# RWKV-7 chunk products on whole 128x128 tiles of TensorE, and a shorter top-k bit step

## The chip, the cores and the metric

The kernel runs on one core of one Trainium2 chip. The metric is the device time of one execution in microseconds (us); the figure given is a median over runs of the same program.

## What is computed

One layer of a hybrid encoder, for a prompt of 1024 frames and a sample of 64 frames with history. One projection of the normed input (1024 columns to 5836) feeds three branches: A, RWKV-7 time mixing with 8 heads of 64; B, forgetting attention with 8 heads; C, sparse attention whose top-k keys are picked by an indexer. The gated branches are projected back and added. The change touches branch A and the top-k of branch C. Branch A is, per head and frame:

```python
def step(S, inp):
    r_t, w_t, k_t, v_t, kk_t, a_t = inp
    sa = jnp.einsum('bhij,bhj->bhi', S, -kk_t)
    S = (S * w_t[:, :, None, :] + sa[..., None] * (kk_t * a_t)[:, :, None, :]
         + v_t[..., None] * k_t[:, :, None, :])
    return S, jnp.einsum('bhij,bhj->bhi', S, r_t)
```

followed by a group norm per head. Top-k keeps, per query row, the 256 best scores (144 for the sample).

## The kernel before

The kernel is one program in the Tile framework, which orders the instructions of each engine; the source gives the order by generators that are woven together.

The early stage normalises the input, loads constants (`setup`, L270) and runs the indexer, which produces the scores. The projection of every 128 columns (a piece) is `proj` (L148): 8 steps of three matmuls for each of three spans of frames. Weights come by `load_w` (L122): a transfer on SyncE's queue into one of two raw buffers (`NW=2`), a cast by ScalarE, then six GpSimd operations. Pieces are filler: `pump` (L190) advances them by credits after every step of other work. `park_mixed` (L759) is the filler that blends each column with the frame before it, through a row `zs`.

The long stage is branch A. Frames are cut in chunks of 64; a unit is four chunks of one pair of heads. There are 17 units, 16 of the prompt and one of the sample. `braid` (L236) interleaves, for unit u, by the declared step counts: the tail of u-2 (group norm and gate), the chain of u-1, the inverse and the value rows of u, and the preparation of u+1. After every step it pumps 0.7 of a filler step. Beside it top-k advances 17 steps a unit.

In `prepare` the elementwise part (L1268) loads the unit's rows by four transfers, then forms decayed queries and keys (QR, BK). `chunk_rows` (L1359) turns BK, forms the products of keys and queries for each head with a contraction of 64 (L1384) and masks them into BN (the strictly lower part) and BA. `chunk_invert` (L1464) inverts a unit triangular matrix of 64x64 per head and chunk. It doubles the block size five times; a level has one group of whole products (`whole`, L1450) and one or two groups of eight 64x64 products (`each`, L1443), and both the inverse U and its transpose T are updated by VectorE. A last correction step gives UD. `chain` (L1507) walks the four chunks: old state times queries (L1531), UD times that (L1536), both heads' rows copied to UV, the new state (L1544, L1549), and the output rows (L1553, L1555). Each of these is issued once per head, on 64 rows or 64 columns of the array.

`topk` (L546) finds a threshold per row bit by bit, 32 times: four small VectorE operations make the candidate (L581, L570, L571, L583), ScalarE and VectorE count the scores above it, and three more (L591 to L593) settle the bit.

After the stage come the attention branches with the rest of the projections and the output projection as filler. An fp32 matmul appears as two rows in the trace, one for each pass.

## Time and profile before

| What | Value |
| --- | --- |
| Runs | 1340.92 us median of 3 (1340.4 to 1344.45) |
| Profiled execution | 1340.06 us; its span, first to last instruction, 1338.3 us |
| TensorE matmul busy | 1268.5 us, 95% |
| TensorE weight load busy | 966.5 us, 72% |
| VectorE busy | 863.3 us, 65% |
| ScalarE busy | 776.4 us, 58% |
| GpSimd busy | 671.9 us, 50% |
| Mean granted TensorE clock | 0.978 |

Busy time is the union of an engine's rows. A matmul row runs until its modelled end, and rows overlap, so what a matmul costs in the queue is read from the start of one to the start of the next. PEld rows are weight loads and overlap matmuls. A line number is that of the kernel before; a helper's line covers all its callers.

### The profile page before, as it was taken

How to read it: one execution, taken by the hardware profiler on the slowest of the kernel's cores; microseconds unless marked ns; L12 is line 12 of the kernel's file. 1: busy time of each engine (PE TensorE's matmuls, PEld its weight loads, DVE VectorE, ACT ScalarE, POOL GpSimd, SP SyncE). 2: the span in 40 equal slices, each digit the busy share in tenths (PEclk: the TensorE clock that was granted, in tenths of full speed). 3: DMA queues.
4: the chain of work that ended last, by engine and by line, in shares of the span. 5: the costliest groups of instructions: out<-in, count | busy, mean ns of one | idle time of the engine just before them, and what ended most of it. 6: DMA issues, size and time to landing. Idle time of an engine off the chain costs nothing.

```text
span 1338.3 us, 29487 instructions
## 1 busy us (share of the span) xinstructions
PE 1268.5 (95%) x10563; PEld 966.5 (72%) x10563; DVE 863.3 (65%) x2603; ACT 776.4 (58%) x1758; POOL 671.9 (50%) x975
## 2 busy tenths in 40 slices
PE   7799999999999999999899998999999989999997
PEld 5567677777777676677666776888888766777764
DVE  7338437878777777767995316556666489666642
ACT  6234437676777677676353346667665477555532
POOL 6224355454454455555454465656666566444411
PEclk9999999999999899989999999999999989999999
DMA  7351523223223223424232469777664576543323
GB/s 222 68 106 46 152 86 94 66 61 94 62 70 113 91 79 111 144 92 120 69 104 67 155 172 261 223 210 214 181 202 131 169 215 180 138 131 99 99 76 95
DMA packets 172622, 169.61 MB, mean 127 GB/s; under 512 B 38546, under 2 KB 147130, under 8 KB 172475
## 3 DMA queue, kind: packets, MB, share of 16 engines
q1 hardware_dynamic: 172314, 166.89, 43.1%
q8 instruction: 84, 1.38, 0.4%
q0 software_dynamic: 160, 0.82, 0.3%
q14 instruction: 64, 0.52, 0.1%
HBM read 104.61 MB, written 62.24 MB: 125 GB/s over the span
## 4 chain that ended last, share of the span: by engine, by line
PE 72%; DVE 12%; DMA 7%; ACT 3%; issue 3%; POOL 2%; SPq 1%; DVEq 0%; POOLq 0%; ACTq 0%
PE pproj L154 32%; PE pproj L1669 6%; PE ps_pv L966 4%; PE ps_atp L107 4%; PE ps_tp L1669 4%; DMA wraw<-in_w_in_dram 3%; PE ps_ga L1384 3%; PE ps_sc L935 2%; PE ps_sc L936 2%; PE ps_gb L1443 2%; PE ps_gc L1553 1%; PE ps_tp L107 1%; PE ps_gb L1450 1%; PE ps_gc L1555 1%; ACT junka L587 1%
## 5 line engine op out<-in xcount | busy, mean ns | idle before, releaser
L154 PE MATMUL pproj<-uH,wh 128*128 128x384 f32 (+4 forms) x1088 | 496.5, 456 | 0.0
L154 PE MATMUL pproj<-uH,wl 128*128 128x384 f32 (+4 forms) x1088 | 364.7, 335 | 0.0
L154 PE MATMUL pproj<-uL,wb 128*128 128x384 bf16 (+4 forms) x1088 | 360.8, 332 | 0.0
L154 PEld LDWEIGHTS pproj<-uH,wh 128*128 128x128 f32 (+1 forms) x1088 | 218.4, 201 | 4.1
L154 PEld LDWEIGHTS pproj<-uH,wl 128*128 128x128 f32 (+1 forms) x1088 | 209.2, 192 | 2.1
L154 PEld LDWEIGHTS <-wb 128*128 128x128 bf16 (+1 forms) x1088 | 106.8, 98 | 116.9 <-issue 80.2
L587 ACT ACTIVATE junka<-score,tk_ntau 128x1024 f16<-128x1024 f32 (+4 forms) x160 | 149.3, 933 | 42.3 <-DVE tk_ntau L583 21.6
L887 POOL TENSOR_SCALAR S<-S,mx 128x128 f32<-128x128 f32 (+8 forms) x136 | 102.7, 759 | 83.3 <-DVE mx L886 63.2
L140 POOL TENSOR_TENSOR wl<-wraw,wh 128x256 fp32r<-128x256 f32 (+1 forms) x184 | 138.0, 780 | 10.5 <-ACT wh L137 9.9
L905 DVE TENSOR_TENSOR hl<-ps_atp,hl 128x512 fp32r<-128x512 f32 (+3 forms) x184 | 109.4, 600 | 51.0 <-ACT hl L904 49.4
L904 ACT CAST hl<-ps_atp 128x512 fp32r<-128x512 f32 (+3 forms) x184 | 93.1, 514 | 68.9 <-PE ps_atp L107 61.8
L882 ACT ACTIVATE S<-S,mx 128x128 f32<-128x128 f32 (+8 forms) x136 | 105.7, 778 | 44.9 <-DVE mx L878 40.4
L142 POOL TENSOR_SCALAR wb<-wraw 128x512 bf16<-128x512 f32 (+1 forms) x92 | 61.4, 683 | 126.9 <-issue 57.2
L966 PE MATMUL ps_pv<-hl,VS 128*128 128x256 f32 (+3 forms) x640 | 113.9, 291 | 5.8 <-ACT hl L904 2.5
L966 PEld LDWEIGHTS ps_pv<-hl,VS 128*128 128x128 f32 (+1 forms) x640 | 89.6, 175 | 18.9 <-ACT hl L904 3.6
L107 PE MATMUL ps_atp<-ident,S 128*128 128x128 f32 x616 | 102.7, 277 | 0.4 <-POOL S L887 0.2
L1132 POOL TENSOR_TENSOR cb<-nm,T 128x256 f32<-128x256 bf16 (+2 forms) x80 | 51.5, 649 | 62.7 <-DVE mx L878 52.7
L107 PEld LDWEIGHTS ps_atp<-ident,S 128*128 128x128 f32 x616 | 75.4, 142 | 5.7 <-POOL S L887 0.6
L1669 PE MATMUL pproj<-oh,gh 128*128 128x512 f32 x144 | 69.3, 500 | 0.4 <-ACT pproj L1717 0.3
L137 ACT CAST wh<-wraw 128x1024 fp32r<-128x1024 f32 (+1 forms) x46 | 47.7, 1037 | 34.8 <-PE pproj L154 28.0
L776 DVE SCALAR_TENSOR_TENSOR zm<-pproj,omm,zs 128x384 f32<-128x384 f32 (+2 forms) x52 | 25.8, 495 | 45.5 <-ACT zs L775 42.3
L1669 PE MATMUL pproj<-ol,gb 128*128 128x512 bf16 (+1 forms) x144 | 52.8, 387 | 1.7 <-DVE ol L1649 1.7
(377 smaller groups left out, 2889.5 us busy)
## 6 DMA issues: line engine op xcount, KB each, us to landing
wraw<-in_w_in_dram SPq DMA_DIRECT2D x45, 512.0 KB
oraw<-in_w_out_dram SPq DMA_DIRECT2D x12, 512.0 KB
out_dram<-rows SPq DMA_DIRECT2D x10, 512.0 KB
x<-in_x_prompt_dram SPq DMA_DIRECT2D x8, 512.0 KB
wt<-a_wa SPq DMA_DIRECT2D x16, 256.0 KB
b_v<-vs SPq DMA_DIRECT2D x8, 512.0 KB
VS<-b_v SPq DMA_DIRECT2D x8, 512.0 KB
d_y<-y SPq DMA_DIRECT2D x64, 64.0 KB
```

The source lines that it names most:

```text
L107: self.nc.tensor.transpose(out, x, self.ident[:n, :n])
L140: nc.gpsimd.tensor_tensor(l[:, k:k + 2, :n], raw[:, k:k + 2, :n], h[:, k:k + 2, :n], op=OP.subtract)
L142: nc.gpsimd.tensor_scalar(b[:, k:k + 4, :n], raw[:, k:k + 4, :n], 1.0, 0.0, op0=OP.mult, op1=OP.add)
L154: self.nc.tensor.matmul(ps[:n, :nt], a[:, k, :n], b[:, k, t0:t0 + nt], start=(k == 0 and i == 0), stop=(k == KD - 1 and i == 2))
L587: nc.scalar.activation(junk[:, :sc.shape[1]], sc, AF.Sign, bias=ntf[:, j:j + 1], accum_out=cnt[:, j:j + 1])
L882: nc.scalar.activation(S[:, :kn], S[:, :kn], AF.Exp, bias=mx[:, nm - 1:nm], scale=-1.0, accum_out=mx[:, 6:7])
L887: nc.gpsimd.tensor_scalar(S[:, :kn], S[:, :kn], mx[:, 7:8], 0.5, op0=OP.mult, op1=OP.mult)
L904: nc.scalar.copy(ph[:kr, a:b], ps[:kr, a:b])
L905: nc.vector.tensor_tensor(pl[:kr, a:b], ps[:kr, a:b], ph[:kr, a:b], op=OP.subtract)
L966: nc.tensor.matmul(pv[0:m, q0:256], VS[:, kb, 0:m], hl[:, x, o:o + w], start=kb == 0 and x == 0, stop=at[-1][0] == last and n == 3)
L1132: nc.gpsimd.tensor_tensor(o, x, y, op=OP.add)
L1669: nc.tensor.matmul(ps[hf][:n, :], parts[m // 4][q][:, m % 4, :n], self.wo[m][q // 2][:, hf * 512:hf * 512 + 512], start=m == 0 and q == 0, ...
```

## The change

Both heads of a pair are placed on the diagonal of one 128x128 stationary tile (zeros elsewhere), so that one whole product replaces two on halves. For that there are three QB buffers and U0, zeroed once, and masks of 128 columns. The inverse keeps only U and turns it after each level by a product with an identity (`transposed`), so it yields 18 times instead of 14. The chain issues one product for the old state, one for the inverse, two for new state and output rows together, one for the output part of the old state; the state is then updated per half, and the output rows are added per half at the end. Value rows and the tail turn two chunks at once. A unit's four loads can be issued while the unit before is prepared (`elem_loads`, `ahead`), with one buffer for `wt` and `zt`. There is one raw weight buffer (`NW=1`), with a separate one for the first piece. `park_mixed` works in rows of one span and fetches the last column of the span before from its projection bank. Top-k keeps the threshold in sign-corrected form and settles a bit in three operations. The value-row product (L1429) stays on 64x64 tiles.

```diff
@@ load_w
-        raw = self.wraw.tile([P, KD, P], F32, tag="raw", name="wraw")
+        pool, wide, x = (self.wsp, P, "") if self.loaded else (self.ip, n, "0")
+        raw = (self.wraw if self.loaded else pool).tile([P, KD, wide], F32, tag="raw" + x, name="wraw")
...
-NW=2
+NW=1
@@ setup
+            for con, a, b in ((xa, 0, D), (xc, D, C_M)):
+                nc.sync.dma_start(out=con[:, :b - a], in_=I["consts"][:, a:b])
+                nc.vector.tensor_copy(self.con[:, a:b], con[:, :b - a])
...
+            for c in (slice(0, 64), slice(64, P)):
+                nc.sync.dma_start(out=lrows[0:8, c], in_=I["a_lnx_w"].rearrange("x (a p) -> (x a) p", p=64))
+                nc.sync.dma_start(out=lrows[8:16, c], in_=I["a_lnx_b"].rearrange("x (a p) -> (x a) p", p=64))
@@ topk
         for b in range(31, -1, -1):
-            bit = 1 << b
-            v.tensor_scalar(cand, cur, bit if b < 31 else -2147483648, None, op0=OP.bitwise_xor)
-            to_float(cand)
-            v.tensor_scalar(ntau, tau, -2147483648, None, op0=OP.bitwise_xor)
             for j in range(na):
...
-            v.tensor_tensor(ge, cnt, k1, op=OP.is_ge)
-            v.tensor_scalar(t1, ge, float(bit) if b < 31 else -2147483648.0, None, op0=OP.mult)
-            v.tensor_tensor(cur, cur, t1, op=OP.bitwise_xor)
+            v.tensor_tensor(ge, cnt, k1, op=OP.is_lt)
...
+                v.tensor_scalar(t1, ge, float(1 << b), float(1 << b - 1 if b else 0), op0=OP.mult, op1=OP.add)
+                v.tensor_tensor(tau, tau, t1, op=OP.bitwise_xor)
@@ park_mixed
+        last = None
         for t0, n in CHUNKS:
             ps = yield from self.proj(w, t0, n)
+            zs = self.zs.tile([P, 388], F32, tag="zs", name="zs")
+            if last is None:
+                v.memset(zs[:, 0:1], 0.0)
+            else:
+                nc.scalar.activation(zs[:, 0:1], last, AF.Copy, scale=mu)
+            last = ps[:, n - 1:n]
@@ prepare, elem
         yield from self.elem(self.one, slots, x)
+        if after and all(f"a{hp}" in self.filled for hp, _ in after):
+            self.ahead = self.elem_loads(after)
         yield from self.chunk_rows(self.one, x)
...
+        rb = tile("e1", "rb")
+        sc.copy(rb.rearrange("p (x o) -> p x o", x=4), rn.rearrange("p (x o) -> p x o", o=1).broadcast_to([P, 4, 64]))
         for b in range(2):
-            for h in range(2):
-                rb = rn[:, 2 * b + h:2 * b + h + 1].broadcast_to([P, 64])
-                nc.tensor.matmul(ps[halves[h], b * P:b * P + P], rb, self.ident, start=True, stop=True)
+            nc.tensor.matmul(ps[:, b * P:b * P + P], rb[:, b * P:b * P + P], self.ident, start=True, stop=True)
...
+        for h in range(2):
+            v.tensor_tensor(BK[hv[h], :, h], r3(tha)[hv[h]], Pi[hv[h]], op=OP.mult)
+            g.tensor_tensor(BK[hv[h], :, 1 - h], r3(kp)[hv[h]], Pi[hv[h]], op=OP.mult)
+            v.tensor_tensor(QB[hv[h], :, 1, h], kk[hv[h]], Pt[hv[h], :, 0:64], op=OP.mult)
+            g.tensor_tensor(QB[hv[h], :, 0, 1 - h], r3(r)[hv[h]], Pt[hv[h], :, 1:65], op=OP.mult)
@@ chunk_rows
+        for c0 in (0, 2):
             ps = G()
+            for c in (0, 1):
+                nc.tensor.matmul(ps[:, 256 * c:256 * c + 256], BK[:, c0 + c].rearrange("p a t -> p (a t)"),
+                                 QB[:, c0 + c].rearrange("p x h t -> p (x h t)"), start=True, stop=True)
+            q = ps.rearrange("p (c x h t) -> p x h c t", c=2, x=2, h=2)
+            for i, dst in ((1, BN[:, :, c0:c0 + 2]), (0, A[:, :, 2 * c0:2 * c0 + 3:2])):
+                for h in range(2):
+                    v.tensor_tensor(dst[:, h], q[:, i, h], am[:, i].broadcast_to([P, 2, 64]), op=OP.mult)
@@ chunk_invert
+        def thin(*pairs):
+            ps = G()
             for c in range(4):
                 for i, (l, r) in enumerate(pairs):
+                    nc.tensor.matmul(ps[:, c * 64:c * 64 + 64], l(c), r(c), start=i == 0, stop=i == len(pairs) - 1)
...
+        def wide(l, r):
+            ps = G()
+            for c in range(4):
+                nc.tensor.matmul(ps[:, c * P:c * P + P], flat(l[:, c]), flat(r[:, c]), start=True, stop=True)
...
         for lv in range(5):
+            Y = on_diagonal(thin((nd[0], lambda c: T[:, c])), C_LV + 128 * lv)
             yield
-            if lv < 4:
-                pt = each(at(U), at(Y))
-                T2 = t16("T16", 2)
-                v.tensor_tensor(T2, T, pt, op=OP.subtract)
-                T = T2
-            pu = each(at(Y), at(U))
-            U2 = t16("U16", 2)
+            pu = wide(Y, U)
+            U2 = diag("U16", bufs=2)
             v.tensor_tensor(U2, U, pu, op=OP.subtract)
             U = U2
             yield
+            T = transposed(U)
+            yield
@@ chain
-            for h in range(2):
-                nc.tensor.matmul(pa[hv[h]], QR[hv[h], c, 1], S[hv[h]], start=True, stop=True)
+            nc.tensor.matmul(pa, flat(QB[:, c, 1]), S, start=True, stop=True)
...
+            nc.tensor.matmul(pb, flat(UD[:, c]), za, start=True, stop=True)
...
             for h in range(2):
+                nc.tensor.matmul(ch[:, h, c], BA[:, h, c], UV[:, h, c], start=True, stop=True)
...
             for h in range(2):
+                v.scalar_tensor_tensor(self.state[hv[h]], ch[hv[h], h, c], Pt[hv[h], c, 64:65], sp[hv[h]], op0=OP.mult, op1=OP.add)
+            nc.tensor.matmul(ab[:, 256 + c * 64:320 + c * 64], flat(QB[:, c, 0]), S, start=True, stop=True)
...
+        sc.copy(Yt, ab[:, 256:512].rearrange("p (c t) -> p c t", t=64))
+        for h in range(2):
+            o = hv[1 - h]
+            v.tensor_tensor(Yt[o], ch[o, h], Yt[o], op=OP.add)
@@ program
-                work.append(("invert", s.chunk_invert(s.one, x[u]), 14, ()))
+                work.append(("invert", s.chunk_invert(s.one, x[u]), 18, ()))
```

## Rows read from the trace of the kernel before

**Rows 1.** Stages: us, then busy us (count) of each engine, clock, DMA.

```profile
166.00:433.00 267.00, 261.39 (x2942) 197.19 (x2942) 196.10 (x679) 176.99 (x404) 133.82 (x212) 1.00 0.28 82
433.00:646.00 213.00, 201.09 (x2251) 150.08 (x2243) 160.99 (x509) 146.60 (x342) 115.80 (x175) 0.96 0.34 106
```

**Rows 2.** One line's view, the copy that ends each unit's chain.

```profile
L1559 ACT COPY Yt<-ps_gc x17: 365/372/373, 251.2 to 774.7; 128x256 f32<-128x256 f32 x17
```

**Rows 3.** TensorE's waits, 172 to 776 us: total, times, longest.

```profile
PE ps_gc L1553 <- DVE S L1549: 8.1, 14, 2.5
PE ps_gb L1443 <- DVE Y L1481: 3.0, 5, 0.9
```

**Rows 4.** TensorE's timeline, 301 to 308 us: start, length, what, count.

```profile
300.58 0.59 PE L1393 MATMUL ps_ga<-rk,ones 128*128 128x256 f32 x2
301.11 0.34 PE L1544 MATMUL ps_gc<-UV,BA 128*64 128x64 f32 x4
301.37 0.31 PE L1443 MATMUL ps_gb<-Y,U 64*64 64x64 f16 x8
...
301.74 0.34 PE L154 MATMUL pproj<-uL,wb 128*128 128x384 bf16 x1
...
303.12 0.34 PE L1553 MATMUL ps_gc<-UV,BA 128*64 128x64 f32 x4
...
303.66 0.61 PE L1303 MATMUL ps_ga<-ones,k 128*128 128x2 f32 x4
304.12 0.28 PE L1450 MATMUL ps_gb<-T,ND 128*128 128x64 f16 x4
304.24 0.33 PE L154 MATMUL pproj<-uL,wb 128*128 128x384 bf16 x1
...
305.63 0.34 PE L154 MATMUL pproj<-uH,wl 128*128 128x384 f32 x1
305.90 0.33 PE L1536 MATMUL ps_gd<-za,UD 64*64 64x64 f32 x4
306.06 0.29 PE L1443 MATMUL ps_gb<-U,Y 64*64 64x64 f16 x8
306.29 0.34 PE L154 MATMUL pproj<-uL,wb 128*128 128x384 bf16 x1
...
306.63 0.33 PE L154 MATMUL pproj<-uH,wl 128*128 128x384 f32 x1
306.81 0.60 PE L107 MATMUL ps_ga<-ident,QR 128*128 128x128 f32 x4
307.24 0.33 PE L154 MATMUL pproj<-uL,wb 128*128 128x384 bf16 x1
```

**Rows 5.** The same timeline elsewhere: first departure, a score group, last departure.

```profile
174.39 0.66 PE L1335 MATMUL ps_ga<-ident,arn 128*64 128x128 f32 x8
...
327.80 1.16 PE L1384 MATMUL ps_ga<-QR,BK 64*128 64x128 f32 x8
328.88 0.33 PE L1536 MATMUL ps_gd<-za,UD 64*64 64x64 f32 x4
...
775.87 0.27 PE L107 MATMUL ps_tp<-ident,kT 128*64 128x128 f32 x1
```

**Rows 6.** VectorE's groups by shape, 250 to 600 us: busy us, mean ns.

```profile
L1481 DVE TENSOR_TENSOR Y<-ps_gb,con 128x256 f16<-128x256 f32 x54 | 22.7, 420 | 5.4 <-PE ps_gb L1450 4.9
...
L1549 DVE SCALAR_TENSOR_TENSOR S<-ps_gc,Pt,sp 128x64 f32<-128x64 f32 x42 | 11.7, 279 | 7.3 <-PE ps_gc L1544 7.1
...
L581 DVE TENSOR_SCALAR tk_cand<-tk_cur 128x8 int32<-128x8 int32 x25 | 6.5, 259 | 0.5
```

**Rows 7.** ScalarE's groups by shape, the same stretch.

```profile
L1495 ACT COPY T<-ps_gb 128x256 f16<-128x256 f16 x10 | 3.6, 362 | 1.9 <-PE ps_gb L1457 1.8
```

**Rows 8.** The chain that ended last, 50 to 90 us: start, length, what.

```profile
57.06 30.84 DMA wraw<-in_w_in_dram
```

**Rows 9.** ScalarE's timeline, 44 to 100 us.

```profile
88.00 1.04 ACT L137 CAST wh<-wraw 128x1024 fp32r<-128x1024 f32 x1 [6.42 <-DMA wraw<-in_w_in_dram]
```

More of the change, by code (lines that the diff above doesn't have):

```diff
@@ L50 @@
 C_LV = C_SCAN + 260
-C_U2 = C_LV + 5 * 64
+C_OB = C_LV + 5 * 128
+C_U2 = C_OB + 128
 C_I64 = C_U2 + 64
@@ new lines, in transposed, with on_diagonal @@
+        def transposed(U):
+            T = one.tile([P, 4, 64], F16, tag="T16", name="T16", bufs=2)
+            sc.copy(T, thin((lambda c: flat(U[:, c]), lambda c: self.i64h[:, 0])))
+            return T
+        def on_diagonal(ps, mask):
+            Y = diag("Y16")
+            m = con[:, mask:mask + P].rearrange("p (h t) -> p h t", h=2)
+            v.tensor_tensor(Y, ps.rearrange("p c (o t) -> p c o t", o=1).broadcast_to([P, 4, 2, 64]),
+                            m.rearrange("p (o h) t -> p o h t", o=1).broadcast_to([P, 4, 2, 64]), op=OP.mult)
+            return Y
@@ L1492, in chunk_invert @@
             yield
-        T = t16("T16", 2)
-        sc.copy(T, transposed(U))
+            T = transposed(U)
+            yield
+        R = on_diagonal(thin((nd[0], lambda c: T[:, c]), (nd[1], lambda c: T[:, c]), (lambda c: self.identh, lambda c: T[:, c]),
+                             (lambda c: self.identh, lambda c: self.i64h[:, 1])), C_OB)
         yield
-        R = t16("Y16")
-        eye = self.identh.rearrange("p (o t) -> p o t", o=1).broadcast_to([P, 4, P])
-        v.tensor_tensor(R, bcast(con[:, C_I64:C_I64 + 64]), whole((ND[:, 0], T), (ND[:, 1], T), (eye, T)), op=OP.subtract)
-        yield
-        UD = one.tile([P, 4, 64], F32, tag="UD", name="UD", bufs=2)
-        v.scalar_tensor_tensor(UD, U, -1.0, each(at(R), at(U)), op0=OP.mult, op1=OP.subtract)
+        UD = diag("UD", F32, 2)
+        v.tensor_tensor(UD, wide(R, U), U, op=OP.subtract)
         x.update(UD=UD)
@@ L1534, in chain @@
             yield
-            for h in range(2):
-                nc.tensor.matmul(pb[hv[h]], UD[hv[h], c], za[hv[h]], start=True, stop=True)
+            nc.tensor.matmul(pb, flat(UD[:, c]), za, start=True, stop=True)
             for h in range(2):
```

231 lines of the change are left out of this document (111 added, 120 removed).

## The prediction, made before the change was run

> **What bounds the kernel now.** I read the sums by stage first, then one stage closely, then who waits for whom. From 166 to 776 us the eight-head RWKV work runs beside the projections that are pumped in as filler, and TensorE is busy 261 of 267 us up to 433 and 201 of 213 us up to 646; VectorE has 196 and 161, ScalarE 177 and 147 [rows 1]. All the edits that run often lie in this stage. Its 17 units end between 251.2 and 774.7 us, 16 steps of 32.7 us [rows 2]. TensorE's queue is in order, and the longest wait in it is the chain's second product on the new state, 8.1 us in all [rows 3]. So the stage is paid in TensorE time: start to start, not the length of a row. VectorE, at three quarters, is next.
>
> **Leaving the whole-array shape costs time.** A filler matmul gives way to another 128x128 one after 0.18 us (306.63 to 306.81), and to a 64x64 one after 0.27 (305.63 to 305.90): 0.09 us for a departure [rows 4]. I count 275 in the timeline, first and last as shown [rows 5], 16 a unit: 1.5 us.
>
> The Trainium skill, TensorEngine Tiling (Array Packing), Key Properties, says that a change of tiling mode drains the engine; that is the 0.09. The same page, The Problem, speaks against this change: a contraction of 64 underuses the full array and should be packed. It is a rival below.
>
> **TensorE, term by term, per unit.** Old: the chain takes four steps, each with the state product 0.26 (301.11 to 301.37), the output product and the two products of the old state 0.54 (303.12 to 303.66), and the inverse times the row 0.16, or 0.27 where the shape changes behind it (305.90 to 306.06; L1544's equal four passes take 0.26); in the middle 4 x 1.015 = 4.06. The inverse: four levels of 16 small products at 0.37, four groups of eight at 0.23 (last level, UD, two transposes), 32 whole products with 64 columns at 0.03 (304.12 to 304.24): 3.36. The two score groups take 1.08 each: 2.16 [rows 5]. Eight turns at 0.11 (306.81 to 307.24): 0.86. With departures 11.9 us.
>
> New: a chain step has five fp32 products, each of two passes as now. No row has a whole-tile fp32 pass with 64 columns. From below, L1303's pass with 2 columns takes 0.115 (303.66 to 304.12, four); from above, L1393's with 256 takes 0.22 (0.53 less a departure, halved). By columns the value lies near the lower row; I take 0.115: 4 x 10 x 0.115 = 4.6. The inverse: 11 thin groups at 0.12, 16 thin products at 0.03, six wide groups of four with 128 columns, between a thin group's 0.12 and the 0.43 of four fp32 turns of 128 columns, by columns 0.24: 3.24. Scores: four products of 256 columns at 0.44, and one 0.09: 1.85. Four turns: 0.43. Sum 10.1. The difference, 1.8 x 17, is **31 us**; if the doubtful terms all go against it (wide groups at 0.43, the old 0.16, scores at 0.53) it is 3, and with wide groups at 0.12 it is 43. The row-norm broadcast also shrinks, from eight passes to four; left at nothing.
>
> **Filler.** The inverse yields 18 times instead of 14, and each yield pumps 0.7 of a filler step of 0.52 us (306.29 to 306.81): 17 x 2.8 x 0.52 = 25 us come into this stage and leave later ones, where TensorE is also full. Net nothing; if the later stages then wait for softmax instead, up to 5 us is lost.
>
> **VectorE.** 256 columns out of PSUM cost 0.42, 64 cost 0.28 [rows 6], so 512 about 0.61 and 128 about 0.33. Inverse: ten ops grow by 0.19, four of 0.42 go, three more grow: +0.8. Chain: the state update becomes two ops, +1.1; two adds for Yt, +0.8; four masked products become eight, +0.9. Top-k loses four of seven small ops a bit, one of them 0.26 [rows 6], 32 bits: -33 us, 2.9 a unit over the 11 units that have bits (six yields a bit, 17 a unit). Sum +0.7 a unit; after the bits end, +3.6. VectorE goes from about 0.75 to about 0.8 of a unit. Four of those freed ops stood between two bits of ScalarE's counts, so ScalarE waits less there. ScalarE gets four more copies of 0.36 [rows 7], the row-norm copy and smaller pieces, some +2.3 us; GpSimd four products of half height, below 3 us. Both have the room: hidden, unless their queue is what the inverse waits for.
>
> **Waits that go and come.** The output product no longer follows the new state: up to 8.1 us go [rows 3]; I take 5. What is late next is the inverse: its serial handoffs rise from 14 to 18, each with TensorE, then VectorE or ScalarE, and all TensorE work queued behind waits along. From nothing to 18 x 0.1 us a unit, 31 us; I take 12. Yt's copy and adds now hold both chain banks, so the next unit's first product waits for them; other steps stand between: nothing, at worst 17 copies of 0.37 [rows 2], 6 us. A projection bank of a mixed piece is held until ScalarE has read its last column, after the next chunk: 26 times nothing to 0.36 [rows 7], filler queued behind; I take 3 of 9 us. Unit loads (four transfers, on SP) are issued a unit ahead; the longest waits of TensorE are on VectorE [rows 3], not on loads, so no gain is taken.
>
> One raw weight buffer instead of two: a load starts when the previous conversion ends, and SP holds whatever stands behind it. A piece is 24 filler steps of 0.52, at least 12.5 us of TensorE and more with the other work between, and its cast takes 1.04 [rows 9]: hidden in the long stage, I estimate. Early it is not. The load issued at 57.06 landed 30.84 us later, and ScalarE stood 6.4 us at its head, up to 88.00 [rows 8, 9]. Now that late load is one piece earlier in the order, so filler that ran before 88 must wait: from nothing, if other work is ahead of the cast in ScalarE's queue, to the rest of the 30.84, 24 us; I take 7. The setup's split constant load and doubled norm rows cost fractions of a microsecond beside the input normalisation: nothing.
>
> **Sum.** -31 - 5 + 12 + 3 + 7 = -14, and -4 for the clock: the granted clock averaged 0.96 of its upper level (2.4 GHz) from 433 to 646, where TensorE idled 12 us [rows 1], and 0.04 of 213 us is 8.5, half of which I expect back with fewer drains. -18 against the profiled execution's 1340.06 (its span is 1338.3) gives 1322; the median of the runs shown is 0.9 higher, so 1322 to 1323. I give **1322**, its own range 1306 to 1336.
>
> **Rivals.**
> Slower: the inverse's ladder sets the pace. It decides where a handoff exceeds 1.87 us: 18 of them then pass 32.7 plus the 0.94 that moved filler (25) less early and bank waits (10) pays back over 16 steps. Today's mean spacing is 32.7 / 14 = 2.34 us, but filler sets that, not the handoff. At 2.0: 16 x (36.0 - 32.7) = 53, less 25, plus 10: +38, **1378**. For it: VectorE and ScalarE are fuller and the handoffs longer (0.61 against 0.42). Against: TensorE waits for the inverse only a few us now [rows 3]. Chance 0.20.
>
> No change: the early stop is the whole 24 us. ScalarE's queue is in order, so a cast put early blocks score work. -18 + 17 = -1: **1339**. For: 30.84 us [rows 8]; against: the cast may stand late in the queue. Chance 0.15.
>
> Slower by lost packing: if a whole pass of 64 columns costs the 0.22 of 256 columns, the chain grows 4.2 us a unit, 71 us: **1393**; it decides from 0.14 a pass. Only the 2-column row [rows 4] speaks against, but it is near. Chance 0.05. The skill's packing rule, above, points this way.
>
> Faster by more: handoffs cost nothing and all of the 8.1 goes: -31 - 8 - 4 + 5 = -38, down to **1302**, and 1290 with 43 for the first term. Chance 0.18. The forecast keeps 0.42.
>
> **Numbers.** Less than 0.3% (4 us) cannot be told from no change. Faster: forecast and the better case, 0.60 together, 0.60: what the forecast's edge loses to no change, the second rival's better half returns. No change: most of the second rival, 0.14. Slower: both slow rivals, 0.26 with what edges in. Range 1290 to 1358: it leaves out some 0.05 below and most of the slow rivals' far side, 0.15 above.
>
> **What would show it.** Right: nearly no 64x64 rows but value_rows' product; chain step passes 0.11 apart; three top-k ops between counts; unit step 31 to 33 us with more filler in it; ScalarE's first long stand before 88 us longer. Wrong: passes over 0.14; TensorE waiting tens of us on Y16, U16 or T16; unit steps over 34 us; a projection waiting for wraw after 166 us.

## The result: 1433 us, and the profile after

The changed kernel takes **1433.28 us** (median of 4 runs, 1432.97 to 1433.99) where the kernel before takes 1342.43 beside it (1340.4 to 1344.45): ratio **1.069**, 95% interval 1.065 to 1.072, slower. The span grew from 1338.3 to 1430.9 us. The forecast was 1322 with a range to 1358.

First the same two stretches as [rows 1], with the early one ahead of them, in the view by stages of after (columns as there):

```profile
50.00:100.00 50.00, 28.99 (x135) 20.37 (x133) 5.94 (x13) 8.70 (x19) 9.12 (x15) 0.76 0.45 74
...
166.00:433.00 267.00, 225.94 (x1841) 180.91 (x1840) 194.38 (x558) 178.57 (x437) 139.70 (x211) 0.98 0.25 74
433.00:646.00 213.00, 185.25 (x1574) 152.78 (x1573) 177.76 (x497) 153.28 (x375) 122.44 (x182) 0.98 0.32 101
```

The same view further on:

```profile
1100.00:1200.00 100.00, 76.76 (x418) 61.38 (x416) 62.36 (x233) 58.51 (x154) 56.83 (x96) 0.78 0.57 152
```

TensorE is no longer full: 226 of 267 us where it was 261, 185 of 213 where it was 201. VectorE is no fuller than before up to 433, so it has not become the bound by its share. Between 50 and 100 us, and again after 1100, TensorE idles, with the granted clock at 0.76 and 0.78.

The view of the line that ends each unit's chain (Yt's copy, now L1601) answers to [rows 2]:

```profile
L1601 ACT COPY Yt<-ps_gd x17: 372/373/375, 271.0 to 855.8; 128x256 f32<-128x256 f32 x17
```

The first unit ends 20 us later, the 16 steps take 36.55 us each instead of 32.72 (61 us in all), and from the last unit to the end it is 575 us instead of 564. These three make the 92.6 us of span.

TensorE's waits in the long stage, 271 to 856 us, answer to [rows 3]:

```profile
PE ps_gb L1507 <- DVE Y L1518: 20.5, 23, 2.6
PE ps_gb L1501 <- DVE U L1537: 18.4, 21, 3.6
PE ps_ga L111 <- DVE BK L1390: 5.3, 4, 2.6
PE ps_gb L1501 <- ACT T L1512: 5.3, 10, 1.2
```

All of the inverse's three links (Y, U and T) now hold TensorE, 44 us of waits in all. In the same view of before, over its own stage (251 to 775 us), they hold it 11 us, and the longest wait was the 8.1 us on the new state. The early stop is one row of ScalarE's timeline, 50 to 100 us (start, length, what, and in brackets the idle time ahead of it and what ended it):

```profile
87.83 1.04 ACT L141 CAST wh<-wraw 128x1024 fp32r<-128x1024 f32 x1 [27.66 <-DMA wraw<-in_w_in_dram]
```

and two of SP's, 40 to 62 us:

```profile
49.50 0.29 SPq L1260 DMA_DIRECT2D d_t<-t5v  x1
57.81 6.45 SPq L136 DMA_DIRECT2D wraw<-in_w_in_dram  x1
```

ScalarE stands 27.66 us for a weight, where it stood 6.42 [rows 9]. The load is issued at 57.81, 8 us behind a 1.5 MB write (the bias table, d_t<-t5v), and its issue alone takes SP 6.45 us.

**What of the steps can be seen directly.** TensorE's timeline, start and length as in [rows 4]:

```profile
299.79 0.28 PE L1597 MATMUL ps_gd<-S,QB 128*128 128x64 f32 x1
299.90 0.39 PE L1507 MATMUL ps_gb<-U,Y 128*128 128x128 f16 x4
300.12 0.30 PE L158 MATMUL pproj<-uL,wb 128*128 128x320 bf16 x1
...
301.56 0.29 PE L1501 MATMUL ps_gb<-i64h,U 128*128 128x64 f16 x4 [0.29 <-DVE U L1537]
...
303.55 0.28 PE L1501 MATMUL ps_gb<-T,ND 128*128 128x64 f16 x4
303.67 0.33 PE L158 MATMUL pproj<-uL,wb 128*128 128x384 bf16 x1
303.70 0.47 PE L158 MATMUL pproj<-uH,wh 128*128 128x384 f32 x1
304.00 0.34 PE L158 MATMUL pproj<-uH,wl 128*128 128x384 f32 x1
305.35 0.40 PE L1507 MATMUL ps_gb<-U,Y 128*128 128x128 f16 x4 [1.01 <-DVE Y L1518]
305.58 0.33 PE L158 MATMUL pproj<-uL,wb 128*128 128x384 bf16 x1
...
307.39 0.33 PE L1576 MATMUL ps_gd<-S,QB 128*128 128x64 f32 x2
307.56 0.28 PE L1501 MATMUL ps_gb<-i64h,U 128*128 128x64 f16 x4
```

A whole-tile fp32 pass of 64 columns takes 0.11 us (299.79 to 299.90) or 0.085 (two in 307.39 to 307.56); the wide group takes 0.22 and 0.23, the thin group 0.12. So TensorE's prices were taken well. What was not is the wait, as in the hole of one microsecond ahead of 305.35.

VectorE's price for 512 columns out of PSUM stands in its groups by shape, 250 to 600 us (as [rows 6]), with the three top-k operations that are left between two bits:

```profile
L1518 DVE TENSOR_TENSOR Y<-ps_gb,con 128x512 f16<-128x512 f32 x57 | 39.1, 686 | 5.9 <-PE ps_gb L1501 4.8
L1537 DVE TENSOR_TENSOR U<-U,ps_gb 128x512 f16<-128x512 f16 x48 | 32.8, 683 | 2.3 <-PE ps_gb L1507 1.5
...
L601 DVE TENSOR_TENSOR tk_ge<-tk_cnt,tk_k 128x8 f32<-128x8 f32 x28 | 7.4, 264 | 1.9 <-ACT junka L597 1.6
L611 DVE TENSOR_TENSOR tk_tau<-tk_tau,tk_t 128x8 int32<-128x8 int32 x28 | 7.2, 256 | 0.6
L610 DVE TENSOR_SCALAR tk_t<-tk_ge 128x8 int32<-128x8 f32 x28 | 7.0, 248 | 0.6
```

### The profile page after: what moved, and what is told of

Read it like the earlier page. It is cut to its first block, busy times and chain, and to the rows that moved or that the text cites. A ratio compares the mean times of both kernels' runs of the same rounds, so it can differ in the third digit from the quotient of the medians.

```text
span 1430.9 us, 26365 instructions
## 1 busy us (share of the span) xinstructions
PE 1261.3 (88%) x8863; PEld 999.8 (70%) x8863; DVE 929.0 (65%) x2588; ACT 813.4 (57%) x1918; POOL 718.1 (50%) x1030
## 5 line engine op out<-in xcount | busy, mean ns | idle before, releaser
L158 PE MATMUL pproj<-uH,wh 128*128 128x384 f32 (+4 forms) x1088 | 502.9, 462 | 0.0
L158 PEld LDWEIGHTS <-wb 128*128 128x128 bf16 (+1 forms) x1088 | 110.8, 102 | 108.0 <-issue 83.5
L597 ACT ACTIVATE junka<-score,tk_tau 128x1024 f16<-128x1024 f32 (+4 forms) x160 | 149.7, 935 | 57.1 <-DVE junk L591 24.0
L1518 DVE TENSOR_TENSOR Y<-ps_gb,con 128x512 f16<-128x512 f32 x102 | 69.9, 686 | 12.3 <-PE ps_gb L1501 10.7
L1507 PE MATMUL ps_gb<-U,Y 128*128 128x128 f16 x408 | 40.8, 223 | 28.6 <-DVE Y L1518 27.0
```

Source lines behind the costliest of these rows:

```text
L158: self.nc.tensor.matmul(ps[:n, :nt], a[:, k, :n], b[:, k, t0:t0 + nt], start=(k == 0 and i == 0), stop=(k == KD - 1 and i == 2))
L597: nc.scalar.activation(junk[:, :sc.shape[1]], sc, AF.Sign, bias=tf[:, j:j + 1], accum_out=cnt[:, j:j + 1])
L1518: v.tensor_tensor(Y, ps.rearrange("p c (o t) -> p c o t", o=1).broadcast_to([P, 4, 2, 64]), m.rearrange("p (o h) t -> p o h t", o=1).broad ...
```

## The experiments

The table takes each run's numbers from the same three views: the time, the end of the first unit and the mean of the 16 unit steps (the copy of Yt), and busy us in the stage between first and last of them (the view by stages). Filler steps are the records of the projections in the stage divided by three. The last column is the granted TensorE clock in the stage, as a share of its upper level (2.4 GHz). A handoff is a step of the inverse after which TensorE's next product needs what VectorE or ScalarE has just made.

```
run                                 us  first  step  stage     PE  idle  DVE  filler  clock
before                          1342.4  251.2  32.7  523.5  498.5  25.0  388     481   0.97
after                           1433.3  271.0  36.6  584.8  505.8  79.0  448     531   0.97
e1 old inverse                  1359.3  259.6  32.8  525.5  482.7  42.8  427     486   0.96
e2 long ladder, in before       1388.9  254.7  35.5  568.6  521.6  47.0  378     488   0.96
e3 after, less filler           1426.4  271.9  36.3  580.7  497.0  83.7  446     485   0.94
e4 after, write from GpSimd     1431.8  273.9  36.4  582.1  503.7  78.4  448     531   0.97
e5 one raw buffer, in before    1367.4  263.6  33.0  527.4  502.9  24.5  388     481   0.96
e6 top-k, in before             1334.5  247.7  32.4  517.7  498.1  19.6  374     483   0.97
e7 14 handoffs, GpSimd hop      1400.6  263.9  35.2  563.9  497.8  66.1  428     487   0.95
e8 old inverse, wide ops        1391.6  262.1  34.7  554.9  495.7  59.2  472     485   0.94
e9 old inverse, 18 handoffs     1423.6  267.4  36.5  583.7  506.6  77.1  414     486   0.94
e10 after, short write          1412.3  242.6  36.7  587.2  507.6  79.6  448     531   0.97
e11 before, top-k, short wr.    1319.6  233.1  32.3  516.1  495.1  21.0  373     483   0.98
e12 e1, short write             1334.1  234.7  32.9  526.1  481.2  44.9  426     486   0.96
e13 transposes unwaited         1362.9  259.4  33.0  528.2  483.2  45.0  449     526   0.98
e14 inverse unwaited            1373.6  261.4  33.6  537.3  491.7  45.6  443     523   0.98
e15 14 handoffs, whole tiles    1370.9  260.8  33.8  540.4  486.9  53.5  447     481   0.97
e16 e15, short write            1353.7  237.1  33.6  537.7  483.6  54.1  448     481   0.97
```

The kernel before stood at 1340 to 1348 on the five chips of these runs, and its single runs spread over some 14 us on a chip (1340 to 1354 over 13 runs on one). A kernel timed once is therefore good to some 10 us; e6, e11, e12 and e16 were run several times, the others once. The clock differs too: e3, e7, e8 and e9 ran the stage at 0.94 or 0.95, most that they are held against at 0.96 or 0.97, and how many of their microseconds are the clock's is not separated.

### First four: the inverse, the ladder alone, the filler, the queue of the write

**e1**: after, with the inverse of before (the edit is shortened: the loop over the levels stands as one line, tiles and masks are left out).

```diff
-    for lv in range(5): Y = on_diagonal(thin(...)); yield; U -= wide(Y, U); yield; T = transposed(U); yield
+    for lv in range(5): Y = whole(ND, T) * mask; yield; T -= each(U, Y); U -= each(Y, U); yield
-    work.append(("invert", s.chunk_invert(s.one, x[u]), 18, ()))
+    work.append(("invert", s.chunk_invert(s.one, x[u]), 14, ()))
```

> The changed kernel with the inverse of the kernel before (64x64 products, 14 steps, U and its transpose updated side by side), its result written per half onto the diagonal of UD; everything else as changed. Theory 1 (the inverse's serial handoffs, 18 with 512-column operations between, set the pace of the long stage and its extra four yields pull filler in): the steps between unit ends fall from a mean of 36.6 us to 31 to 33, filler in them from 531 steps back to about 480, TensorE's waits on Y, U and T from 51 us to under 15, time 1340 to 1375 us. Rival (the fuller VectorE from chain, scores and masks holds the stage): unit steps stay at 35 us or more, time over 1400 us.

1359.33, in the theory's range. The whole-tile inverse accounts for 74 of the 91 us; what is left, +16, is the early stop and the rest.

**e2**: before, with a ladder of 18 handoffs on its 64x64 tiles: the transposed copy is no longer updated beside the inverse but transposed from it at each level, and filler is scaled by 39/43 to stay in its stage.

```diff
-            if lv < 4:
-                pt = each(at(U), at(Y))
-                T2 = t16("T16", 2)
-                v.tensor_tensor(T2, T, pt, op=OP.subtract)
-                T = T2
...
             U = U2
             yield
-
-        T = t16("T16", 2)
-        sc.copy(T, transposed(U))
-        yield
+            T = t16("T16", 2)
+            sc.copy(T, transposed(U))
+            yield
...
```

> The kernel before, old shapes, but the inverse keeps only U and turns it after each level: 18 handoffs instead of 14, VectorE does four operations of 0.41 us a unit less, ScalarE four copies of 0.36 more; filler per step scaled by 39/43 so that a unit holds as much as before. Theory 1 (the number of handoffs counts by itself): 20 to 50 us slower than before, TensorE's waits on Y, U and T from 11 to over 30 us. Rival (only what stands in a handoff, the 512-column operations at 0.69 us, counts): within 10 us of before.

1388.85, with VectorE emptier (378 against 388 us) and TensorE idle 22 us longer. A longer ladder alone slows the kernel before, with narrow operations. TensorE is also busy 23 us longer in the stage (521.6 for 498.5), so not all of the 45 us need be waiting.

**e3**: after, filler rate times 39/43.

```diff
-            s.braid(work, ... R_A / 10, ...)
+            s.braid(work, ... R_A / 10 * 39 / 43, ...)
```

> The changed kernel with filler per step scaled by 39/43, so that the long stage holds about 480 steps of it again instead of 531. Theory 2 (moving filler forward left a stretch of attention with none, 76 us between the last projection and the first output projection against 19 before): that gap shrinks below 40 us and what follows the last unit takes 25 us of filler more and 35 to 40 less of waiting, so the whole is 10 to 35 us faster than the changed kernel, the larger figure if unit steps shorten too. Rival (filler placement is neutral): within 8 us of the changed kernel, the long stage shorter by 25 and the rest longer by 25.

1426.38, below the theory's gain of 10 to 35 us: the stage loses 46 filler steps and gets only 4 us shorter. Either they had run in time in which TensorE idled anyway, or the lower clock of this run (0.94 for 0.97) took the gain; that is open. In after, filler runs out at 1114 us and the next projections of the output start at 1190.6; in this run it lasts to 1158. Moved filler costs 7 us, by one run.

**e4**: after, the 1.5 MB write issued from GpSimd's queue instead of SP's.

```diff
-            nc.sync.dma_start(out=self.d_t5.rearrange("q h r -> h q r"), ...)
+            nc.gpsimd.dma_start(out=self.d_t5.rearrange("q h r -> h q r"), ...)
```

> The changed kernel with the 1.5 MB write of the relative bias table issued from GpSimd's queue instead of SyncE's. Theory 3 (the early loss of some 20 us is the weight load stuck behind that write, now one piece earlier because of the single raw buffer): ScalarE's stand of 27.7 us before the cast near 60 us falls below 8, the first unit ends at 250 to 256 us instead of 271, time 1410 to 1418 us. Rival (the early loss comes from the longer setup or the single buffer as such): first unit end stays at 265 or later, time within 6 us of the changed kernel.

1431.75, no help: ScalarE still stands 28.57 us, up to 88.15. Which of the two queues issues the write does not matter. SP's issue of the load takes 0.39 us here instead of 6.45, so the long issue in after is not what costs. The Trainium skill, DMA: Bandwidth & Descriptors, Issuing engines are not separate DMA queues, says that transfers issued by different engines run on the same transfer engines; this run agrees.

### Four more: the parts of the change one by one

**e5**: before, with one raw weight buffer.

```diff
-        raw = self.wraw.tile([P, KD, P], F32, tag="raw", name="wraw")
+        pool, wide, x = (self.wsp, P, "") if self.loaded else (self.ip, n, "0")
+        raw = (self.wraw if self.loaded else pool).tile([P, KD, wide], F32, tag="raw" + x, name="wraw")
...
-NW=2
+NW=1
```

> The kernel before, with the weight loading of after alone: one raw weight buffer instead of two, the first weight piece raw in a pool of its own. Theory (the early stop is the single buffer beside the 1.5 MB table write): ScalarE stands 20 to 28 us for the early weight instead of 6.4, the first unit ends at 262 to 268 instead of 251, and the time rises by 8 to 18 us, to 1351 to 1361. Rival (the single buffer costs nothing by itself; the late first unit of after comes from the stretched setup and the longer ladder): first unit at 250 to 254 and 1341 to 1346.

1367.43, 24.5 us over before and above the theory's 1351 to 1361. ScalarE's timeline has the stand of after:

```profile
86.88 1.04 ACT L136 CAST wh<-wraw 128x1024 fp32r<-128x1024 f32 x1 [28.44 <-DMA wraw<-in_w_in_dram]
```

The unit step hardly moves (33.0): in the long stage the one buffer is hidden, as predicted; early it is not. The first unit ends 12 us later, the stage takes 4 us more, and what follows it 11 us more (575 us for 564). These 11 I cannot put down to the buffer: as much filler is left for the end as in before, and e6, with both buffers, has 572 us there.

**e6**: before, with the new top-k (its part of the change's diff).

> The kernel before, with the top-k of after alone. Theory (TensorE sets the stage and VectorE's seven small operations a bit are mostly cover): 1333 to 1344, unit step 32.2 to 32.8. Rival (the ScalarE counts stand behind those operations and hold the stage): 1320 to 1332. A rise above 1348 would be against both.

1334.54, ratio 0.995 (0.992 to 0.998): 8 us gained on the path, at the edge of the theory's range.

**e7**: after, with the transposed copy kept beside the inverse, 14 handoffs; VectorE's masked product is stacked (256 columns), GpSimd puts it on the diagonal.

```diff
-            Y = on_diagonal(thin((nd[0], lambda c: T[:, c])), C_LV + 128 * lv)
...
+            v.tensor_tensor(Ys, thin((nd[0], lambda c: T[:, c])), m, op=OP.mult)
...
+            for h in range(2):
+                g.tensor_scalar(Yd[hv[h], :, h], Ys[hv[h]], 1.0, 0.0, op0=OP.mult, op1=OP.add)
             yield
-            pu = wide(Y, U)
...
+                sc.copy(T2, thin((lambda c: self.identh, lambda c: T[:, c]), (lambda c: flat(U[:, c]), lambda c: Ys[:, c])))
...
+            pu = wide(Yd, U)
...
```

> After, with its whole-tile inverse, but the transposed copy of the inverse kept beside it level by level, so that no level waits for a transpose: 14 handoffs instead of 18. VectorE's product of a level has 256 columns instead of 512, its difference still 512, and GpSimd puts the product on the diagonal. Theory (the number of serial handoffs sets the pace): 1360 to 1385, unit step 33 to 34.5, waits of TensorE for Y and U together below 20 us. Rival (the width of VectorE's operations sets it, 512 columns at 0.69 us for 256 at 0.42): one of the two wide operations a level stays, so half of the 74 us stays, 1395 to 1410.

1400.55: the rival's number. But it adds a GpSimd hop to each level, so this one does not separate the two; e15 does.

**e8**: e1 with VectorE's operations of the inverse doubled to 512 columns (`twice` writes the same result two times; one of its three uses is shown).

```diff
-            v.tensor_tensor(Y, whole((ND[:, 0], T)), bcast(...), op=OP.mult)
+            twice(Y, whole((ND[:, 0], T)), bcast(...), OP.mult)
```

> The old 64x64 inverse in the kernel of after, as in the first experiment (1359), with its VectorE operations doubled to 512 columns by computing each result twice: 14 handoffs, every one with the wide operation of after. Theory (number of handoffs): 1359 to 1375, since 14 handoffs stay 14 and each is only some 0.2 us longer. Rival (width of the operations): VectorE gets 15 x 0.27 us a unit, 69 us over 17 units, and the time goes to 1400 to 1430.

1391.6, between the two: 32 us for some 62 us of VectorE's operations (14 x 0.26 x 17), part of it perhaps the clock's. Width does cost something where VectorE is at 0.85, which no other kernel here but e13 reaches.

### The last corner, and the write

**e9**: e1 with 18 handoffs, by the same edit as e2.

> The first experiment (after with the old 64x64 inverse, 14 handoffs, narrow operations: 1359), with the inverse transposing at every level as after does: 18 handoffs, operations still of 256 columns, filler scaled by 39/43 so that the stage holds as much of it. It is the fourth corner of a square: 14 narrow 1359, 14 wide 1392, 18 wide 1426 (after with the same filler). Theory (the two costs add: four more handoffs and the wide operations each lengthen the inverse's queue of waits): 1389 to 1402. Rival (only the two together hurt, as slack is used up first): 1360 to 1375, and the corner 18 wide is more than the sum. Rival (the count alone is enough and the width adds nothing on top): above 1415.

1423.6, against the theory of adding costs and in the second rival's range: 18 handoffs with narrow operations are as slow as 18 with wide ones (1426, e3, at the same clock of 0.94). But its transposes are 64x64 visits that after has not, so the square is not a clean one.

**e10**: after, the table written for 16 query rows instead of 128, and read back in eight pieces for each half.

```diff
-        self.d_t5 = self.dram.tile([P, 8, 384], F32, tag="d_t5", name="d_t5")
+        self.d_t5 = self.dram.tile([16, 8, 384], F32, tag="d_t5", name="d_t5")
-                nc.sync.dma_start(out=t, in_=bass.AP(..., offset=z.offset + 127 + 384 * h, ap=[[8 * 384 - 1, P], [384, 4], [1, 256]]))
+                for o in range(0, P, 16):
+                    nc.sync.dma_start(out=t[o:o + 16], in_=bass.AP(..., offset=z.offset + 127 - o + 384 * h, ap=[[8 * 384 - 1, 16], [384, 4], [1, 256]]))
...
```

> After, with the bias table written to DRAM for 16 query rows instead of 128 (0.2 MB instead of 1.5 MB) and read back by 16 transfers instead of two; the outputs stay what they are. Theory (the single raw buffer costs 24 us because the load that it delays meets the 1.5 MB write in the transfer engines): ScalarE's stand before 90 us falls from 27.7 to below 12, the first unit ends at 255 to 262 instead of 271, and the time to 1412 to 1422. Rival (the single buffer costs a load's own latency at every early piece whatever else is in flight): stand stays above 20 us, 1428 to 1436.

1412.25, 21 us gained, at the lower end of the theory's 1412 to 1422; the first unit ends at 242.6, earlier than its 255 to 262. Its rows are to be held against those of after. ScalarE's timeline, 50 to 100 us:

```profile
61.14 1.05 ACT L141 CAST wh<-wraw 128x1024 fp32r<-128x1024 f32 x1 [0.85 <-DMA wraw<-in_w_in_dram]
```

SP's, 40 to 62 us:

```profile
57.15 0.39 SPq L136 DMA_DIRECT2D wraw<-in_w_in_dram  x1
```

The view by stages:

```profile
50.00:100.00 50.00, 50.00 (x291) 36.71 (x289) 29.78 (x72) 25.36 (x54) 20.18 (x29) 1.00 0.42 102
```

The load, issued at nearly the same moment, is there for ScalarE after 4 us (57.15 to 61.14) instead of 30, TensorE is busy all of the 50 us, and the first unit ends 28 us earlier.

**e11**: before, with the top-k of after and this short write (edits as shown).

> The kernel before with the top-k of after and the short table write, two raw buffers, old shapes everywhere else: the candidate for the fastest. Theory: ScalarE's 6.4 us stand for the early weight goes as well, 1324 to 1333. Rival (the early stand is covered and only the top-k counts): 1333 to 1338, as the top-k alone. The 16 reads in place of two could cost SP some us later; above 1338 they do.

**1319.6, ratio 0.982 (0.978 to 0.986)**: the fastest version found, and below the theory's 1324 to 1333. Two raw buffers and old shapes; the long write costs the kernel before 15 us as well (1334.5 to 1319.6).

**e12**: e1 with the short write.

> After with the old 64x64 inverse (1359 in the first experiment) and the short table write: what the whole-tile chain and score products are worth where neither the early stop nor the long ladder stands against them. Theory (early stop gone, chain and scores bring next to nothing because VectorE's extra operations take their place): 1338 to 1348, first unit at 248 to 254. Rival (the whole-tile chain gains the 1.1 us a unit that its products save): 1318 to 1330.

1334.08, ratio 0.992 (0.990 to 0.995), between the theory's range and the rival's. Beside e11 it is 14 us slower, though TensorE works 14 us less in the stage (481 against 495): the saved work came back as idle time, 45 against 21 us. Its one raw buffer is hardly the reason any more: the first units end at 234.7 and 233.1 us. So the rest of the change, the whole-tile chain and scores among it, brings nothing and costs up to 14 us; which part of it costs them was not tried.

### Waits or work: the dependence taken away

**e13**: after, each level transposing the inverse of the level before. All instructions, sizes and filler stay; the result is not the inverse.

```diff
-            U = U2
             yield
             T = transposed(U)
+            U = U2
             yield
```

> After with the same instructions, sizes and filler, but each level transposes the inverse as it stood a level earlier, so TensorE's transposing products no longer follow the difference that VectorE has just made: one of the three serial handoffs of a level is gone (12 left of 17 between the steps), and no work. The result is therefore not the inverse. Theory (serial handoffs, closely spaced, hold TensorE): a third of the 40 to 74 us goes, 1395 to 1415, waits on U below 5 us. Rival (the whole-tile inverse costs what its work costs, the wide VectorE operations above all): 1426 to 1436, and the waits move to Y.

1362.94: **70 of the 74 us are gone**, more than the theory asked for. Of the 17 handoffs between a unit's 18 steps five were taken away: 70 / (5 x 17) = 0.83 us each. TensorE's waits by line, 190 to 850 us:

```profile
PE ps_gb L1507 <- DVE Y L1518: 14.0, 20, 2.0
PE ps_gd L1576 <- DVE S L1595: 7.7, 7, 3.6
...
PE ps_gb L1501 <- ACT T L1512: 1.5, 3, 0.8
...
PE ps_gb L1501 <- DVE U L1537: 0.5, 1, 0.5
```

The waits on U and T have all but gone, and those on Y, which the edit does not touch, fell as well. Not every wait went: the chain's next product on the new state (L1576) stands 7.7 us, where after has 1.9.

**e14**: as e13, with the thin products on the older transposed copy, and the wide products on a finished tile in place of Y.

```diff
-        T = transposed(U)
+        T = T0 = transposed(U)
...
-            Y = on_diagonal(thin((nd[0], lambda c: T[:, c])), C_LV + 128 * lv)
+            Y = on_diagonal(thin((nd[0], lambda c: T0[:, c])), C_LV + 128 * lv)
+            T0 = T
...
-            pu = wide(Y, U)
+            pu = wide(ND[:, 1].rearrange("p c (h t) -> p c h t", h=2), U)
...
```

> As the run before, and also the thin products read the transposed copy of a level earlier and the wide products take a finished tile in place of the masked product: the same instructions and sizes again, but no level waits for the step just before it. Only the order of the queues is left, and the result is not the inverse. Theory (handoffs): 1355 to 1375, that is the old inverse's 1359 within its early stop, unit step 32 to 33.5, TensorE's waits for Y, U and T together below 10 us. Rival (work and width): 1415 to 1436. In between, the share that stays above 1359 is the share of the work.

1373.62, in the theory's range but no gain over e13, and the waits are not below 10 us as the theory asked. What is left of TensorE's longer waits stands mostly at the thin products, on VectorE's Y and U:

```profile
PE ps_gb L1501 <- DVE Y L1518: 11.3, 12, 2.7
PE ps_ga L111 <- DVE BK L1390: 6.8, 8, 2.1
PE ps_gb L1501 <- DVE U L1538: 6.3, 10, 1.5
```

The thin products read neither; the inverse's two PSUM banks are shared, so I take these as waits for a bank, which no run here shows. The 11 us between e13 and e14, one run each, I leave open.

**e15**: a version that does compute the inverse, with whole tiles, wide operations and 14 handoffs.

```diff
             yield
+            if lv < 4:
+                T2 = one.tile([P, 4, 64], F16, tag="T16", name="T16", bufs=2)
+                sc.copy(T2, thin((lambda c: self.identh, lambda c: T[:, c]), (lambda c: flat(U[:, c]), lambda c: Y[:, c, 0]),
+                                 (lambda c: flat(U[:, c]), lambda c: Y[:, c, 1])))
+                T = T2
             pu = wide(Y, U)
...
-            T = transposed(U)
-            yield
+        T = transposed(U)
+        yield
...
```

> After, whole tiles and wide VectorE operations as they are, outputs as they should be, but the transposed copy is kept level by level: T + U^T Y is summed in PSUM in three thin products a chunk (the identity with T, U with either half of the masked product) and copied by ScalarE beside the wide product, so 14 handoffs in place of 18, with four wide operations fewer for nothing else and no GpSimd hop. Theory (waits of the serial chain, which the run without the wait on U put at 70 us): 1355 to 1375, unit step 32.5 to 33.7, filler in the stage back to about 486. Rival (the earlier whole-tile version at 14 handoffs took 1401 because of its wide operation and not because of its GpSimd hop): 1390 to 1410.

1370.86, in the theory's range and 62 us below after, with VectorE as busy as there (447 against 448 us). Part of the 62 is filler, of which the stage now holds 481 steps for 531. Held against e3, which has 485, it is 56 us: 56 / (4 x 17) = 0.82 us for each of the four handoffs a unit, as in e13.

**e16**: e15 with the short write.

> The run before with the short table write: all of the change that helps, without the long ladder and without the early stop. Theory: 21 to 25 us below the run before, 1332 to 1352, so level with the kernel before to a few us faster. Rival (the whole-tile products' saving of TensorE work shows in full once nothing waits): 1305 to 1325, below the 1320 of the old shapes with top-k and short write.

1353.65, ratio 1.009 (1.006 to 1.012), just above the theory's range, and 34 us behind e11. With both losses out, the whole-tile shapes are still no gain: the whole-tile inverse at 14 handoffs costs 20 us over the old one (e16 against e12), the rest up to 14 (e12 against e11).

## Why the prediction was wrong

The measured parts are +74 for the whole-tile inverse (after less e1) and +16 for all else (e1 less before). Of the 74, the four handoffs are 56 (e3 less e15), filler 7 (after less e3), and 11 are what the whole-tile inverse costs without them (e15 less e1; 20 by e16 and e12, which were run several times). Of the 16, top-k is -8 (e6), which leaves 25 for the single buffer and the rest, chain and scores among it. By e5 alone the buffer is 24.5 and the rest 0. With the short write the rest is 14 (e12 less e11, several runs each) and the buffer 10: that write gains 25 us with one buffer (e1 to e12) and 15 with two (e6 to e11). The first unit of e5, 12 us late, speaks for the second split; the runs do not settle it.

**TensorE's work fell about as predicted, and that did not matter.** "The difference, 1.8 x 17, is 31 us." In e13, where the whole-tile work is all there and waits less, TensorE's busy time in the stage without the projections is 483.23 - 309.66 = 173.6 us; before it was 498.49 - 289.17 = 209.3. The view by stages, of before:

```profile
251.20:774.70 523.50, 498.49 (x5630) 371.93 (x5629) 388.31 (x1259) 326.73 (x764) 267.94 (x402) 0.97 0.31 96
```

The same stretch of before, the projections' line alone (TensorE and its weight loads):

```profile
251.20:774.70 523.50, 289.17 (x1447) 182.32 (x1445) 0.97 0.31 96
```

e13, all engines:

```profile
259.40:787.60 528.20, 483.23 (x4241) 408.39 (x4241) 449.44 (x1243) 361.17 (x908) 313.87 (x459) 0.98 0.33 102
```

e13, the projections' line alone:

```profile
259.40:787.60 528.20, 309.66 (x1577) 207.77 (x1578) 0.98 0.33 102
```

After, all engines and the projections' line alone:

```profile
271.00:855.80 584.80, 505.78 (x4283) 416.65 (x4284) 447.60 (x1241) 358.90 (x895) 312.30 (x462) 0.97 0.29 92
271.00:855.80 584.80, 314.84 (x1592) 209.95 (x1593) 0.97 0.29 92
```

That is 36 us less work in e13 and 18 in after (505.78 - 314.84 = 190.9); a row's end is modelled, so these are rough, and the 31 lies between. In neither is the stage shorter. (The term's worst case, given as 3 us, is under 2 by the prediction's own parts; nothing hangs on it.) The step that failed is the first one, "So the stage is paid in TensorE time". TensorE was busy 95% of the stage, but the serial chains fitted in behind its work. With less of it the chains show: e1 has TensorE busy 16 us less than before and idle 18 us more.

**The ladder is the mis-sized term.** "From nothing to 18 x 0.1 us a unit, 31 us; I take 12." Four handoffs a unit cost 56 (e15), at 0.82 us each where the prediction allowed 0.1 for each of 18; five taken away in e13 gave back 70. Two of the prediction's own signs of being wrong came: unit steps over 34 us (36.55) and tens of microseconds of waits on Y, U and T (44). The argument against the slower rival, that "TensorE waits for the inverse only a few us now", read a wait that was small as a handoff that was short. The thing to read was the room, the time between the end of an operand and the start of the product that takes it. Worked out from the records, from the end of VectorE's Y to the next inverse product on TensorE there lay a median of 0.96 us before (12 of 102 under 0.12) and 0.23 in after (46 of 102). From the end of U it was 2.76 us before and 0.36 in after; in the other kernels with 18 handoffs it was 0.73 (e2), 0.55 (e9) and 0.29 (e3), with 14 handoffs, or with a dependence taken away, it was between 1.55 (e14) and 3.09 (e13). Room on U is not the whole account: e8, 32 us slower than e1, has the same 2.10. The first rival, "the inverse's ladder sets the pace", had the mechanism, serial handoffs that hold the queue: it gave 36.0 us a unit at 2.0 us a handoff, and after's unit is 36.55, or 2.03 for each of 18. That the size fits is in part luck: 2.03 is a mean spacing and no measured handoff, and e13 has 1.83 with as many steps. Its time was still 55 us short, because it gave 25 us back through moved filler, and because the early stop was kept for another rival. Two rivals held at once; as cases they had been made exclusive.

**Moved filler was not net nothing.** 49 steps came into the stage, as forecast (17 x 2.8). There they did not fill TensorE's holes, and their lack later left it busy 54 of 76.5 us from 1114 to 1190 at a clock of 0.71:

```profile
1114.10:1190.60 76.50, 53.96 (x278) 44.44 (x277) 46.18 (x188) 44.56 (x126) 44.78 (x82) 0.71 0.55 145
```

By e3, one run, that is 7 us net, where up to 5 was allowed.

**The early stop came whole.** The term went "to the rest of the 30.84, 24 us; I take 7". ScalarE stands 22 us longer in e5 (28.44 for 6.42), the first unit ends 12 us later and the time rises by 10 to 24.5 us, as above. No other work stood ahead of the cast. The row of [rows 8] showed a load of 30.84 us, and the prediction took that as the load's own price without asking what else was in flight; e10 shows that the 1.5 MB write is the reason, e4 that the queue which issues it is not.

**VectorE was costed nearly right.** 512 columns take 0.69 us for an estimated 0.61. Its share in the stage rose from 0.74 to 0.77, for 0.8; in e13, 70 us faster, it is at 0.85. So a full VectorE is not what slowed after. After the top-k has ended it is at 112 of 154 us (646 to 800), 86 before. Top-k's freed operations were overrated: e6 has 17 us less of VectorE's busy time in the whole run (863.3 to 846.2), for 33. They were counted as cover; 8 us lay on the path.

**Smaller terms.** The output product's wait on the new state went, as said: no row of it is left in TensorE's waits. But the next chain step's first product takes the same state, and once the inverse no longer holds the queue it waits 7.7 us (e13), so the 5 us may not have been there to be had. The projection's wait for its bank is 2.5 us, for 3. The clock gave nothing back: it rose from 0.96 to 0.98 from 433 to 646 us, where 4 us were taken, but fell from 1.00 to 0.98 from 166 to 433, and it is 0.97 in the stage in both and lower in the two holes.

**Lost packing** did not happen: it decided from 0.14 us a pass, and passes take 0.085 to 0.11. The Trainium skill, TensorEngine Tiling (Array Packing), The Problem, says that a contraction of 64 or less underuses the full array. No loss by it shows here: TensorE's time without the projections is shorter in e13 and in after.

## What to carry to other kernels

Where an engine is full of interleaved work, ask of every serial chain how much room it has between one handoff and the next, not how long it waits: a chain cut into more handoffs can lose that room on each, and TensorE's saved work then only turns into idle time. To see whether a slow part is waits or work, keep all instructions and take one dependence away. Where a load takes far longer than its like, look for the large transfer that it shares the engines with before removing a buffer that hides it.

## What the runs showed of the hardware

A 0.5 MB load behind a 1.5 MB DRAM write took 30 us, and its issue held SP for 6.45 us; behind a 0.2 MB write it took 4 us and 0.39 (after and e10). With the long write in GpSimd's queue (e4) the issue took 0.39 us and the load still 31. The view of the transfers of after, 40 to 100 us in 40 slices, shows how slowly the engines ran meanwhile: busy share of the 16 transfer engines in tenths, and GB/s, all transfers together.

```profile
DMA  0001000996444445595444444444445100056007
GB/s 0 0 1 33 0 11 8 153 158 114 52 63 57 65 74 95 107 188 72 50 51 49 49 49 49 49 49 50 51 50 150 40 0 0 0 148 201 0 11 175
```

For some 16 us, from 68.5 to 85, they move 50 GB/s with four tenths of their time. The Trainium skill, DMA: Bandwidth & Descriptors, Why a DMA increments its semaphore by 16 and not by 1, says that a transfer takes the largest number of engines up to 16 that divides the outermost dimension of both sides. In this write that dimension is the eight heads, and a share of four tenths fits eight of 16 engines; no run here tried the write with another outermost dimension.

The granted clock is lower where TensorE had holes: from 50 to 100 us it averaged 0.76 of the upper level (2.4 GHz) in after, with TensorE busy 29 of 50 us, and 1.00 in e10, with 50 of 50.

The slower version has the emptier engines: TensorE 0.86 and VectorE 0.77 of the stage in after, 0.91 and 0.85 in e13 with the same instructions.
